# Down projection of a gated decoder block: blocks of 1024 columns, two of eight pairs of k-tiles by Strassen's scheme, the residual in DRAM during the MLP

## The chip, the cores and the metric

The kernel runs on one core of a Trainium2 chip. The metric is the device time of one execution in microseconds. Before the change it is 1585.26 us (median of three runs, 1582.78 to 1585.36). The execution that the profiler recorded took 1583.8 us, and its span, from the first to the last instruction that the profile shows, is 1581.7 us.

## The reference

One decoder layer for 256 tokens of width 2048, all in float32. Its second half, the MLP, is what the change touches; the first half (a combined input projection, three branches with gates, and the projection w_o) ends in the residual `x`.

```
h = RMSNorm_pre(x);  proj = h @ w_in            # conv, short conv, attention query, 3 gates
merged = sum_i sigmoid(gate_i) * y_i            # y_i: a branch's output through its own projection
x = x + RMSNorm_post(merged @ w_o)              # the residual that is kept during the MLP
h = RMSNorm_pre(x)
f = square(relu(h @ w_up)) @ w_down             # w_up 2048 x 8192, w_down 8192 x 2048
x = x + RMSNorm_post(f)
```

## The kernel before

**Precision.** Each float32 operand of a matmul is split into a high part of the type fp32r and a low part (the difference). A product of two tiles takes three matmuls: high by high, high by low, low by high. The split of the activations is made once; the split of the weights is made on the fly for every weight tile, by a copy on ACT into a tile `wh` and a subtraction on DVE into a tile `wl`.

**The weight stream.** All weights pass once, in units of 512 KB, in one fixed order (the list `units`). `fetch_next` issues a unit's DMA on SP into one of six `raw` buffers (`RAW = 6`) and the two instructions that split it into one of five `wh` and five `wl` buffers. `in_unit(u)` fetches up to `LOOK = 4` units ahead of the unit that is being multiplied. A scheduler orders the instructions of each engine when the program is built; the priority of fetches (`PRIO`) and of `soon()` is raised.

**The MLP** runs in four blocks of 2048 of the 8192 hidden columns. In each, four groups of `channels_first` give 512 hidden channels each (the weights are stationary, the tokens move; four PSUM banks per group). DVE and ACT then add the two halves of a bank, apply relu, the norm's factor and the square, and split the result into a tile `ft`. Then four groups of the down projection follow, each of 512 of the 2048 output columns, by `tokens_first`: the tokens are stationary, the weights move, two banks for the two halves of the tokens. `after_down` adds each bank to a sum in SBUF (`acc2`; the first block copies it there on ACT). The last group of the last block is written finer, with the final norm and the output in between.

**Strassen's scheme** is in the kernel already, in `block`, for four of the six gate blocks (`GATES`, with `X_PAIRS`) and for half of w_o (`O_PAIRS`). A block covers 1024 columns, as two halves of 512, and both halves of the tokens, so that each row (a k-tile of 128) takes four products, C11, C12, C21 and C22, in four banks. For a pair of k-tiles it computes seven products in place of eight: P1, P6, P7 and Q5 in four banks of their own, over all pairs of the block, and three that go straight into the C banks. `gather` then adds P1, P6, P7 and Q5 up for the four C results. In the form with pairs the weights of a pair come as four units: "first" and "second" are loaded; "outer" is made from them on DVE by two additions; "inner" is what two accumulating DMAs leave in the buffer of "first", issued on POOL, one after the split of "first" and one after that of "second". `plan_rows` writes out the order of these units among the plain rows, and `TQ` is the order of the four products of a row and of reading out the four C banks.

Of the kernel before, what the change touches and what calls it, by code (L numbers as in the profile page):

```python
# [8 lines left out]
F32 = mybir.dt.float32  # L9
# [6 lines left out]
P = 128  # L16
# [26 lines left out]
X_PAIRS = ((0, 8), (1, 9), (2, 10))  # L43
GATES = ((0, 3), (2, 3), (0, 3))
O_PAIRS = ((0, 4), (1, 5), (2, 6))
TQ = ((0, 1), (0, 0), (1, 1), (1, 0))
LOOK = 4
PRIO = 400
RAW = 6
# [3 lines left out]
def tile_hybrid_block(ctx, tc, x, head, xT, mem, memT, vecs, w_in, w_a_out, w_b_out, w_kv, w_x_out, w_o,  # L53
# [4 lines left out]
    wp = ctx.enter_context(tc.tile_pool(name="wp", bufs=2))  # L58
    big = ctx.enter_context(tc.tile_pool(name="big", bufs=13))
    sm = ctx.enter_context(tc.tile_pool(name="sm", bufs=2))  # L60
    ps = ctx.enter_context(tc.tile_pool(name="ps", bufs=8, space=bass.MemoryType.PSUM))

    uid = [0]

    def name(p):
        uid[0] += 1
        return f"{p}_{uid[0]}"
# [28 lines left out]
            k += s  # L96
        return got

    def plan_rows(w, col0, nk, pairs=(), hold=0):

        taken = [k for p in pairs for k in p]
        rows = [("row", k, None) for k in range(nk) if k not in taken]
        parts = [(4 * j + at, what, k, j) for j, (k0, k1) in enumerate(pairs)
                 for what, k, at in (("first", k0, 0), ("second", k1, 1), ("outer", k0, 4.5), ("inner", k0, 6.5))]
        parts = [p[1:] for p in sorted(parts)]
        order, among = rows[:2], rows[2:-1]
        for n, p in enumerate(parts):
            while n >= hold and among and (len(among) - 0.5) * (len(parts) - hold) >= (len(rows) - 3) * (len(parts) - n):  # L110
                order.append(among.pop(0))
            order.append(p)
        got = []
        for what, k, j in order + among + rows[-1:]:
            units.append((w, k * P, col0, (what, j), None))
            got.append((what, k, j, len(units) - 1))
        return got, pairs

# [162 lines left out]
                    late.pop(0)(acc)  # L281
        return acc

    def block(rows, act, forms=None, sums=None):

        todo = []
        rows, pairs = rows  # L290

        def tile_of(k, t):
            return lambda: [act(k)[:, i, t * P:(t + 1) * P] for i in range(2)]

        def form(j, i):
            return lambda: [f[:, j, i, :] for f in forms]

        for what, k, j, u in rows:
            if what == "row":
# [12 lines left out]
        end = max((i for c, i in last.items() if c[0] != "C"), default=None)  # L312
        acc = {}
        for i, (u, c, a, q) in enumerate(todo):
            wh, wl = in_unit(u)[q]
            ah, al = a()
            first = c not in acc
            if first:
                acc[c] = bank()
            mm(acc[c], ah, wh, first, False)  # L320
            mm(acc[c], ah, wl, False, False)
            mm(acc[c], al, wh, False, i == last[c])
            if i == end:
                with soon():
                    gather(acc, sums)
            if i % 8 == 7:
                between()
        return acc

    def gather(acc, sums):  # L330
        p1, u2 = sums(0, 1), sm.tile([P, NC5], F32, tag="u512", name=name("u"), bufs=2)
        nc.scalar.copy(p1, acc["P1"])
        nc.vector.tensor_tensor(u2, acc["P6"], p1, ALU.add)
        nc.vector.tensor_tensor(sums(1, 1), acc["P7"], u2, ALU.add)
        nc.vector.tensor_tensor(sums(0, 0), acc["Q5"], u2, ALU.subtract)
        nc.vector.tensor_tensor(sums(1, 0), acc["Q5"], sums(1, 1), ALU.subtract)

    def halves(b, dst):
        t = t1k()
# [24 lines left out]

    def lagged(b, w):
        for n in range(2):
            g_gate[b, n] = plan_rows(w_in, C_G + b * D + n * 2 * NC5, KD, X_PAIRS[:GATES[b][n]])
            g_y[b, n] = plan_rows(w, n * 2 * NC5, 8)

    g_sc, g_sx, g_sb = [], [], []  # L370
    lagged(2, w_x_out)
# [3 lines left out]
        g_sb.append(plan(w_in, 0, C_SB + i * NC5))  # L375
    lagged(1, w_b_out)
    lagged(0, w_a_out)
    g_o = [plan_rows(w_o, 0, KD, O_PAIRS, hold=5), None] + [plan(w_o, 0, n * NC5) for n in (2, 3)]
    for blk in range(4):
        for g in range(4):  # L380
            g_up[blk, g] = plan(w_up, 0, blk * D + g * NC5, gain=V_MLP)
        for n in range(4):
            g_dn[blk, n] = plan(w_down, blk * D, n * NC5)


    vec = const.tile([P, V_N], F32, name="vec")
# [255 lines left out]

    def gates(b, n):
        s = t8([P, 2, 2, NC5])
        acc = block(g_gate[b, n], xg, xf, lambda t, q: s[:, t, q, :])
        with soon():
            for t, q in TQ:
                src = acc[f"C{t + 1}{2 - q}"]
                if GATES[b][n]:
                    nc.vector.tensor_tensor(s[:, t, q, :], src, s[:, t, q, :], ALU.add)  # L650
                    src = s[:, t, q, :]
                nc.scalar.activation(s[:, t, q, :], src, AF.Sigmoid, scale=r_of["x"][:, t:t + 1])
        return s
# [169 lines left out]
    def o_part(t, q):  # L823
        return x2[t][:, q * NC5:(q + 1) * NC5]

    acc = block(g_o[0], pair(merged), of, o_part)
    for t, q in TQ:
        nc.vector.tensor_tensor(o_part(t, q), acc[f"C{t + 1}{2 - q}"], o_part(t, q), ALU.add)
        after_o(q, t, o_part(t, q))
# [39 lines left out]


    gq = a_pad.rearrange("p c t -> p (c t)")[:, :D]
    nc.sync.dma_start(gq, g_mlp_post.partition_broadcast(P))
    late_rf = []
    acc2 = [t8([P, D]) for _ in range(2)]

    def after_down(blk, n, t, b, c0=0, c1=NC5):
        b = b[:, :c1 - c0]
        ns = slice(n * NC5 + c0, n * NC5 + c1)
        if blk == 0:
            nc.scalar.copy(acc2[t][:, ns], b)  # L880
            return
        nc.vector.tensor_tensor(acc2[t][:, ns], b, acc2[t][:, ns], ALU.add)
        if blk == 3:
            j = n + (c0 > 0)
            nc.scalar.activation(junk()[:, c0:c1], acc2[t][:, ns], AF.Square, accum_out=ssf[t][:, j:j + 1])
            nc.vector.tensor_tensor(res[t][:, ns], acc2[t][:, ns], gq[:, ns], ALU.mult)

    def finish(t, rf, c0, c1):
        ns = slice(c0, c1)
        nc.vector.scalar_tensor_tensor(res[t][:, ns], res[t][:, ns], rf, x2[t][:, ns], ALU.mult, ALU.add)  # L890
        nc.sync.dma_start(out[t * P:(t + 1) * P, ns], res[t][:, ns])

    for blk in range(4):
        f = []
        for g in range(4):
            first = blk == 0 and g == 0
            if first:
                steps += [stats_2, lambda: over_partitions(r2, r2_bc)]
            banks = channels_first(g_up[blk, g], pair(h2),
                                   late=turns if first else None)  # L900
            ft = t8([P, 4, 2, T], F32R)
            for c, b in enumerate(banks):
                s = t1k()
                halves(b, s)
                nc.vector.scalar_tensor_tensor(s, s, 0.0, r2_bc, ALU.max, ALU.mult)  # L905
                q = t1k()
                nc.vector.tensor_tensor(q, s, s, ALU.mult)  # L907
                split(q, ft[:, c, 0, :], ft[:, c, 1, :])
            f.append(ft)
        if blk == 3:  # L910
            res = [t8([P, D]) for _ in range(2)]
        for n in range(4):
            if blk == 3 and n == 3:
                def none(acc):
                    pass

                def d_0(acc):
                    after_down(3, 3, 0, acc[0])
                    rf = row_rsqrt(ssf[0])
                    for n in range(3):  # L920
                        finish(0, rf, n * NC5, (n + 1) * NC5)
                    late_rf.append(rf)

                def d_1a(acc):
                    after_down(3, 3, 1, acc[1], 0, T)

                def d_1(acc):
                    after_down(3, 3, 1, acc[2], T, NC5)
                    rf = row_rsqrt(ssf[1])
                    with tc.issue_after(mean[0]):  # L930
# [45 lines left out]
```

## Time and profile before

| | value |
|---|---|
| median of 3 runs | 1585.26 us |
| the profiled execution: time, span | 1583.8 us, 1581.7 us |
| busy share of PE, DVE, ACT | 99%, 74%, 51% |
| weights and other data moved | 313.00 MB at a mean of 198 GB/s |
| the MLP | from about 862 us to the end |

PE is the matmul engine, PEld its load of the stationary operand, DVE the vector engine, ACT the scalar engine, POOL and SP the engines that here mostly issue DMAs. A row of a view by windows gives, for a stretch of the span, its length, the busy time of PE, PEld, DVE, ACT and POOL with their instruction counts, the share of full speed of the clock that TensorE was granted, the busy share of the DMA engines, and GB/s. In the view by lines, a group has its busy time, the mean duration in ns of one instruction, and the idle time before them with what ended it. Matmuls overlap, so that the mean duration of one (390 ns) is not its cost; the distance between starts is.

### The profile page before, as it was taken

Reading aid. Unit: us, or ns where it says so; the run is one execution under the profiler, and the core shown is the slowest. Engines: PE = TensorE matmul, PEld = TensorE weight load, DVE = VectorE, ACT = ScalarE, POOL = GpSimd, SP = SyncE. Lnnn points to the kernel's source line nnn. Section 1 sums busy time; section 2 is a strip of 40 time slices with the busy share of each in tenths; the row PEclk is TensorE's granted clock in tenths of the full one; section 3 lists DMA queues with packets and bytes.
Section 4 is the critical chain, followed back from the end, with each engine's and each line's share of the span. In section 5 each row is a group of like instructions: output and inputs, shape, how many; then the busy total and the mean of one; then the engine's idle time right before and its main releaser. Section 6 shows DMA issues by size and latency. Waiting matters only on the chain.

```text
span 1581.7 us, 21250 instructions
## 1 busy us (share of the span) xinstructions
PE 1562.7 (99%) x7908; PEld 1333.9 (84%) x7908; DVE 1164.5 (74%) x1731; ACT 805.8 (51%) x1135; POOL 31.5 (2%) x47
## 2 busy tenths in 40 slices
PE   8999999999999999999999999999999999999997
PEld 7888888888888888888788888888888888888886
DVE  7888787798888987878776775457755676567755
ACT  7654454554443645455455554455534554455542
POOL 0000000000000010000100000000000000000000
PEclk9999999999999999999999999999999999999999
DMA  9765655577666768558775766666556665666562
GB/s 315 223 205 191 189 162 172 160 232 220 186 189 173 237 187 281 183 175 239 225 255 160 213 187 192 195 194 192 187 190 197 188 191 192 190 194 190 188 196 82
DMA packets 142248, 313.00 MB, mean 198 GB/s; under 512 B 9920, under 2 KB 14272, under 8 KB 141632
## 3 DMA queue, kind: packets, MB, share of 16 engines
q1 hardware_dynamic: 138112, 304.30, 61.3%
q0 software_dynamic: 4032, 7.34, 2.7%
q8 instruction: 62, 1.02, 0.3%
q14 instruction: 42, 0.34, 0.1%
HBM read 302.17 MB, written 2.10 MB: 192 GB/s over the span
## 4 chain that ended last, share of the span: by engine, by line
PE 91%; DMA 3%; DVE 3%; issue 2%; ACT 0%; SPq 0%; POOL 0%; POOLq 0%; DVEq 0%; ACTq 0%
PE bank L82 91%; DMA raw<-raw 2%; DVE wl L145 1%; DMA raw<-in_w_in 1%; DMA raw<-in_w_o 0%; DVE t L811 0%; PE bank L769 0%; ACT wh L144 0%; DVE t L665 0%; DVE t L650 0%; DVE t L890 0%; DVE t L345 0%; DVE raw L137 0%; DVE wl L167 0%; PE bank L819 0%
## 5 line engine op out<-in xcount | busy, mean ns | idle before, releaser
L82 PE MATMUL bank<-wh,t 128*128 128x512 f32 (+1 forms) x2564 | 787.5, 387 | 0.0
L82 PEld LDWEIGHTS bank<-wh,t 128*128 128x128 f32 x2564 | 479.8, 188 | 97.1
L82 PE MATMUL bank<-wl,t 128*128 128x512 f32 (+1 forms) x1282 | 496.2, 387 | 0.1
L162 DVE TENSOR_TENSOR wl<-raw,wh 128x1024 fp32r<-128x1024 f32 (+1 forms) x273 | 332.4, 1220 | 208.3 <-ACT wh L161 207.7
L82 PE MATMUL bank<-t,wh 128*128 128x512 f32 (+1 forms) x1936 | 464.1, 390 | 5.8 <-ACT wh L161 4.6
L161 ACT CAST wh<-raw 128x1024 fp32r<-128x1024 f32 (+1 forms) x273 | 286.1, 1049 | 332.2 <-PE bank L82 314.7
L82 PEld LDWEIGHTS bank<-t,wh 128*128 128x128 f32 x1936 | 354.3, 189 | 73.6 <-ACT wh L161 4.6
L144 ACT CAST wh<-raw 128x1024 fp32r<-128x1024 f32 (+1 forms) x188 | 189.4, 1020 | 190.1 <-PE bank L82 117.1
L82 PEld LDWEIGHTS bank<-wl,t 128*128 128x128 f32 x1282 | 241.1, 188 | 49.3 <-DVE wl L145 1.0
L82 PEld LDWEIGHTS bank<-t,wl 128*128 128x128 f32 x1936 | 249.5, 192 | 10.3 <-DVE wl L162 0.7
L82 PE MATMUL bank<-t,wl 128*128 128x256 f32 (+1 forms) x1936 | 252.8, 283 | 0.4 <-DVE wl L162 0.4
L145 DVE TENSOR_TENSOR wl<-raw,wh 128x1024 fp32r<-128x1024 f32 (+1 forms) x188 | 217.8, 1180 | 45.0 <-ACT wh L144 44.3
L167 DVE SCALAR_TENSOR_TENSOR wl<-raw,vec,wh 128x512 fp32r<-128x512 f32 x256 | 180.7, 747 | 78.7 <-ACT wh L166 78.4
L166 ACT ACTIVATE wh<-raw,vec 128x512 fp32r<-128x512 f32 x256 | 171.4, 717 | 106.6 <-PE bank L82 80.3
L574 DVE SCALAR_TENSOR_TENSOR t<-a_pad,vec,t 128x256 f32<-128x256 f32 x240 | 103.6, 478 | 0.0
L340 ACT COPY s<-bank 128x256 f32<-128x256 f32 x128 | 45.8, 366 | 56.0 <-PE bank L82 54.6
L341 DVE TENSOR_TENSOR s<-bank,s 128x256 f32<-128x256 f32 x128 | 51.9, 419 | 20.0 <-ACT s L340 20.0
L344 ACT CAST t<-s 128x256 fp32r<-128x256 f32 x96 | 37.7, 401 | 29.6 <-DVE s L907 21.9
L345 DVE TENSOR_TENSOR t<-s,t 128x256 fp32r<-128x256 f32 x96 | 39.5, 419 | 1.8
L907 DVE TENSOR_TENSOR s<-s 128x256 f32<-128x256 f32 x64 | 27.1, 424 | 1.8
L905 DVE SCALAR_TENSOR_TENSOR s<-s,rm_bc 128x256 f32<-128x256 f32 x64 | 27.0, 422 | 1.4
L439 POOL TENSOR_TENSOR y<-y,mhalf 128x1 f32<-128x1 f32 (+1 forms) x7 | 4.8, 681 | 937.2 <-DVE y L437 937.2
(127 smaller groups left out, 432.7 us busy)
## 6 DMA issues: line engine op xcount, KB each, us to landing
raw<-in_w_in SPq DMA_DIRECT2D x191, 512.0 KB, 4.3
raw<-in_w_up SPq DMA_DIRECT2D x128, 512.0 KB, 3.8
raw<-in_w_down SPq DMA_DIRECT2D x128, 512.0 KB, 4.0
raw<-in_w_kv SPq DMA_DIRECT2D x32, 512.0 KB, 4.5
raw<-in_w_o SPq DMA_DIRECT2D x32, 512.0 KB, 5.3
raw<-in_w_x_out SPq DMA_DIRECT2D x16, 512.0 KB, 4.3
raw<-in_w_b_out SPq DMA_DIRECT2D x16, 512.0 KB, 5.5
raw<-in_w_a_out SPq DMA_DIRECT2D x16, 512.0 KB, 5.0
```

The lines of the kernel that those rows point to most:

```text
L82: nc.tensor.matmul(o, a, b, start=start, stop=stop)
L144: nc.scalar.copy(h[:, part], raw[:, part])
L145: pace[0] = nc.vector.tensor_tensor(l[:, part], raw[:, part], h[:, part].bitcast(F32), ALU.subtract).ins
L161: nc.scalar.copy(h, raw)
L162: pace[0] = nc.vector.tensor_tensor(l, raw, h.bitcast(F32), ALU.subtract).ins
L166: nc.scalar.mul(h[:, j, :], raw[:, j, :], g)
L167: pace[0] = nc.vector.scalar_tensor_tensor(l[:, j, :], raw[:, j, :], g, h[:, j, :].bitcast(F32), ALU.mult, ALU.subtract).ins
L340: nc.scalar.copy(t, b[:, T:])
L341: nc.vector.tensor_tensor(dst, b[:, :T], t, ALU.add)
L344: nc.scalar.copy(dst_h, src)
L345: nc.vector.tensor_tensor(dst_l, src, dst_h.bitcast(F32), ALU.subtract)
L574: nc.vector.scalar_tensor_tensor(conv[:, c, :], src, w, conv[:, c, :], ALU.mult, ALU.add)
```

## The change

In the first three blocks of the MLP both halves of the output columns, and in the fourth block the first half, go through `block` with two pairs of k-tiles each (`D_PAIRS`), so seven blocks of 1024 columns. The plan puts four plain rows ahead of the pairs (`lead=4`). The second half of the last block stays as it was. The sums for the pairs that the activations need (`down_sums`) are made while the second up group of each block is read out; for this two squared tiles of the first group are kept, and their split form takes a large buffer `fd`. To make room, the residual `x2` is written to DRAM at the start of the MLP and read back in the last block. `gather_add` does what `gather` does and adds to `acc2`, which all blocks after the first need. `TQ` changes for every block of the kernel: it now goes through the two halves of the tokens first.

```diff
-TQ = ((0, 1), (0, 0), (1, 1), (1, 0))
+D_PAIRS = ((0, 4), (1, 5))
+TQ = ((0, 0), (1, 0), (0, 1), (1, 1))
...
-    def plan_rows(w, col0, nk, pairs=(), hold=0):
+    def plan_rows(w, row0, col0, nk, pairs=(), lead=2, hold=0):
...
-        order, among = rows[:2], rows[2:-1]
+        order, among = rows[:lead], rows[lead:-1]
...
+    def gather_add(acc, sums):
+        p1, u3 = t512(), t512()
+        nc.scalar.copy(p1, acc["P1"])
+        nc.vector.tensor_tensor(sums(0, 1), acc["P1"], sums(0, 1), ALU.add)
+        nc.vector.tensor_tensor(p1, acc["P6"], p1, ALU.add)
+        nc.vector.tensor_tensor(u3, acc["P7"], p1, ALU.add)
+        nc.vector.tensor_tensor(p1, acc["Q5"], p1, ALU.subtract)
+        nc.vector.tensor_tensor(sums(1, 1), sums(1, 1), u3, ALU.add)
+        nc.vector.tensor_tensor(u3, acc["Q5"], u3, ALU.subtract)
+        nc.vector.tensor_tensor(sums(0, 0), sums(0, 0), p1, ALU.add)
+        nc.vector.tensor_tensor(sums(1, 0), sums(1, 0), u3, ALU.add)
...
-        for n in range(4):
-            g_dn[blk, n] = plan(w_down, blk * D, n * NC5)
+        for n in range(2):
+            if blk < 3 or n == 0:
+                g_dn[blk, n] = plan_rows(w_down, blk * D, n * 2 * NC5, KD, D_PAIRS, lead=4)
+    for n in (2, 3):
+        g_dn[3, n] = plan(w_down, 3 * D, n * NC5)
...
+    def keep_x2():
+        for t in range(2):
+            nc.sync.dma_start(x2_kept[t], x2[t])
...
-        if blk == 0:
-            nc.scalar.copy(acc2[t][:, ns], b)
-            return
...
+    def down_sums(fd, j, qa, qb):
+        s = t512().rearrange("p (i t) -> p i t", i=4)
+        nc.vector.tensor_tensor(s[:, 0, :], qa[:, P:], qb[:, P:], ALU.subtract)
+        nc.vector.tensor_tensor(s[:, 1, :], s[:, 0, :], qa[:, :P], ALU.subtract)
+        nc.vector.tensor_tensor(s[:, 2, :], qa[:, :P], qa[:, P:], ALU.subtract)
+        nc.vector.tensor_tensor(s[:, 3, :], qb[:, :P], s[:, 1, :], ALU.add)
+        split(s, fd[:, 0, j], fd[:, 1, j])
...
+                steps += [stats_2, lambda: over_partitions(r2, r2_bc), keep_x2, load_gq]
...
+                if g == 0 and paired:
+                    kept.append(q)
+                elif g == 1 and paired:
+                    down_sums(fd, c, kept[c], q)
...
         if blk == 3:
             res = [t8([P, D]) for _ in range(2)]
-        for n in range(4):
-            if blk == 3 and n == 3:
+            for t in range(2):
+                x2[t] = t8([P, D])
+                nc.sync.dma_start(x2[t], x2_kept[t])
+        forms = [fd[:, i] for i in range(2)]
+        for n in range(2 if blk < 3 else 1):
+            def part(t, q):
+                return acc2[t][:, (2 * n + q) * NC5:(2 * n + q + 1) * NC5]
+            acc = block(g_dn[blk, n], pair(f), forms,
+                        lambda acc: gather(acc, part) if blk == 0 else gather_add(acc, part))
+            for t, q in TQ:
+                after_down(blk, 2 * n + q, t, acc[f"C{t + 1}{2 - q}"])
+        for n in (2, 3) if blk == 3 else ():
+            if n == 3:
```

The units of one new block stand in this order: four plain rows, first 0, a row, second 0, a row, first 1, a row, outer 0, a row, second 1, inner 0, a row, outer 1, a row, inner 1, two rows.

Three places in the order of the instructions. On DVE, where the down projection of the second block ends and the next block's up projection begins, this stood before (`wl` with `vec` is the split of a w_up unit, L882 the addition of a bank to the sum):

```order
L162 TENSOR_TENSOR wl_10735<-raw_10732,wh_10734 128x1024
L162 TENSOR_TENSOR wl_10753<-raw_10750,wh_10752 128x1024
L167 SCALAR_TENSOR_TENSOR wl_10771<-raw_10768,vec,wh_10770 128x512 x2
L167 SCALAR_TENSOR_TENSOR wl_10791<-raw_10788,vec,wh_10790 128x512 x2
L167 SCALAR_TENSOR_TENSOR wl_10811<-raw_10808,vec,wh_10810 128x512 x2
L167 SCALAR_TENSOR_TENSOR wl_10831<-raw_10828,vec,wh_10830 128x512 x2
L882 TENSOR_TENSOR t_1438_7706<-bank_10694,t_1438_7706 128x512
L882 TENSOR_TENSOR t_1439_7707<-bank_10695,t_1439_7707 128x512
```

And now, at the same place, with `gather_add` in lines 349 to 355 (bank_10847 is P6, bank_10893 P7, bank_10889 Q5; wl_10900 and wl_10917 are the block's last two rows):

```order
L147 TENSOR_TENSOR wl_10900<-raw_10897,wh_10899 128x1024
L349 TENSOR_TENSOR u_10961<-bank_10847,u_10961 128x512
L147 TENSOR_TENSOR wl_10918<-raw_10915,wh_10917 128x1024
L169 SCALAR_TENSOR_TENSOR wl_10930<-raw_10927,vec,wh_10929 128x512 x2
L169 SCALAR_TENSOR_TENSOR wl_10950<-raw_10947,vec,wh_10949 128x512
L350 TENSOR_TENSOR u_10962<-bank_10893,u_10961 128x512
L169 SCALAR_TENSOR_TENSOR wl_10950<-raw_10947,vec,wh_10949 128x512
L351 TENSOR_TENSOR u_10961<-bank_10889,u_10961 128x512
L352 TENSOR_TENSOR t_1439_7710<-t_1439_7710,u_10962 128x512
L354 TENSOR_TENSOR t_1438_7709<-t_1438_7709,u_10961 128x512
L353 TENSOR_TENSOR u_10962<-bank_10889,u_10962 128x512
L169 SCALAR_TENSOR_TENSOR wl_10975<-raw_10972,vec,wh_10974 128x512
```

The reads of P7 and Q5, after which their banks can be written again, stand among the splits of the next up group's first units, and L353 is the last of them.

On SP, in the first up group of the MLP, the DMAs stood so before:

```order
L157 DMA raw_7820<-in_w_up 128x2x512
L157 DMA raw_7844<-in_w_up 128x2x512
L872 DMA a_pad<-in_g_mlp_post 128x2048
L157 DMA raw_7894<-in_w_up 128x2x512
L157 DMA raw_7918<-in_w_up 128x2x512
```

Now two writes of 1 MB each (`x_kept`) stand among them:

```order
L159 DMA raw_7824<-in_w_up 128x2x512
L902 DMA x_kept_7707<-t_1282_6956 128x2048
L159 DMA raw_7848<-in_w_up 128x2x512
L896 DMA a_pad<-in_g_mlp_post 128x2048
L902 DMA x_kept_7708<-t_1284_6959 128x2048
L159 DMA raw_7898<-in_w_up 128x2x512
```

The w_up units behind them are issued later by those two transfers.

On PE, at the start of w_o (from about 773 us), the transposes of the merged branches (`ident`; bank_7011 and bank_7018) stood in two pieces before:

```order
L82 MATMUL bank_7003<-wh_6889,t_1197_6520 128x512
L769 MATMUL bank_7011<-ident,t_654_3545 128x128
L769 MATMUL bank_7018<-ident,t_654_3545 128x128
L82 MATMUL bank_7032<-wh_6907,t_1181_6454 128x512
L82 MATMUL bank_7032<-wl_6908,t_1181_6454 128x512
L82 MATMUL bank_7032<-wh_6907,t_1181_6454 128x512
L769 MATMUL bank_7011<-ident,t_654_3545 128x128 x3
L769 MATMUL bank_7018<-ident,t_654_3545 128x128 x3
```

Now all eight stand together, at the place of the first piece:

```order
L84 MATMUL bank_7005<-wh_6891,t_1197_6522 128x512
L791 MATMUL bank_7013<-ident,t_654_3547 128x128 x4
L791 MATMUL bank_7020<-ident,t_654_3547 128x128 x4
L84 MATMUL bank_7034<-wh_6909,t_1181_6456 128x512
L84 MATMUL bank_7034<-wl_6910,t_1181_6456 128x512
L84 MATMUL bank_7034<-wh_6909,t_1181_6456 128x512
```

With the new `TQ` both halves of the tokens of these columns are read out before the other columns, and the second piece has moved up to the first.

## Rows read from the trace of the kernel before

**Rows 1.** The page: busy time of the engines, and the chain by engine.

```profile
PE 1562.7 (99%) x7908; PEld 1333.9 (84%) x7908; DVE 1164.5 (74%) x1731; ACT 805.8 (51%) x1135; POOL 31.5 (2%) x47
PE 91%; DMA 3%; DVE 3%; issue 2%; ACT 0%; SPq 0%; POOL 0%; POOLq 0%; DVEq 0%; ACTq 0%
```

**Rows 2.** Windows: two paired gate blocks, an up group, a down group.

```profile
312.10:353.60 41.50, 41.44 (x183) 33.99 (x182) 37.49 (x54) 22.50 (x23) 4.47 (x6) 1.00 0.79 226
582.00:623.50 41.50, 41.45 (x184) 33.98 (x183) 36.99 (x39) 24.46 (x27) 2.61 (x3) 1.00 0.86 271
...
922.00:945.00 23.00, 23.00 (x133) 20.29 (x132) 17.78 (x35) 13.02 (x24) 0.00 (x0) 1.00 0.62 195
...
967.00:988.80 21.80, 21.80 (x98) 18.06 (x97) 10.23 (x10) 9.50 (x10) 0.00 (x0) 1.00 0.60 195
```

**Rows 3.** PE in order of time, down projection: start, length, instructions.

```profile
1000.05 0.62 PE L82 MATMUL bank<-wh,t 128*128 128x512 f32 x2
...
1000.73 0.62 PE L82 MATMUL bank<-wh,t 128*128 128x512 f32 x2
```

**Rows 4.** Groups by line and shape: count, busy us, mean ns, idle before.

```profile
L145 DVE TENSOR_TENSOR wl<-raw,wh 128x1024 fp32r<-128x1024 f32 x174 | 208.7, 1220 | 42.9 <-ACT wh L144 42.2
L144 ACT CAST wh<-raw 128x1024 fp32r<-128x1024 f32 x174 | 181.0, 1052 | 167.1 <-PE bank L82 97.4 <-issue 23.0 <-DVE raw L137 15.2
L167 DVE SCALAR_TENSOR_TENSOR wl<-raw,vec,wh 128x512 fp32r<-128x512 f32 x256 | 180.7, 747 | 78.7 <-ACT wh L166 78.4
...
L882 DVE TENSOR_TENSOR t<-bank,t 128x512 f32<-128x512 f32 x23 | 14.9, 683 | 5.9 <-PE bank L82 5.9
...
L145 DVE TENSOR_TENSOR wl<-raw,wh 128x512 fp32r<-128x512 f32 x14 | 9.6, 685 | 2.1 <-ACT wh L144 2.1
L137 DVE TENSOR_TENSOR raw<-raw,raw 128x512 f32<-128x512 f32 x14 | 9.6, 685 | 0.0
...
L447 DVE TENSOR_SCALAR s<-ident,y 128x128 f32<-128x128 f32 x8 | 2.0, 284 | 2.3 <-POOL y L439 1.6 <-POOL y L868 0.7
```

**Rows 5.** The chain in order of time, in the gate block from 312 us.

```profile
325.78 3.56 DMA raw<-in_w_in
329.38 6.16 DMA raw<-raw
...
337.51 243.16 PE bank L82 x1251
```

**Rows 6.** DMAs: the median us to landing is the last number.

```profile
raw<-raw POOLq DMA_DIRECT2D x28, 256.0 KB, 4.1
...
t<-in_x SPq DMA_DIRECT2D x2, 1024.0 KB, 8.8
```

**Rows 7.** The tile raw in the gate block from 312 us: its DMAs.

```profile
DMA to landing us min/median/max: 3.5/4.7/6.2
```

**Rows 8.** PE in order of time at the start of w_o: start, length, wait.

```profile
773.61 0.39 PE L82 MATMUL bank<-wh,t 128*128 128x512 f32 x1
775.55 0.44 PE L769 MATMUL bank<-ident,t 128*128 128x128 f32 x2 [1.55 <-DVE t L665]
...
777.48 1.54 PE L769 MATMUL bank<-ident,t 128*128 128x128 f32 x6 [0.79 <-DVE t L665]
```

**Rows 9.** DVE in order of time at the same place.

```profile
774.82 1.28 DVE L665 TENSOR_TENSOR t<-t,t 128x512 f32<-128x512 f32 x2
...
776.73 0.69 DVE L665 TENSOR_TENSOR t<-t,t 128x512 f32<-128x512 f32 x1
```

**Rows 10.** Windows: the start of w_o, and the start of the MLP.

```profile
777.40:780.80 3.40, 3.32 (x11) 2.94 (x12) 3.40 (x5) 1.59 (x3) 0.61 (x1) 0.50 0.81 193
...
860.00:870.00 10.00, 8.88 (x72) 8.31 (x70) 9.93 (x19) 9.84 (x25) 0.56 (x1) 1.00 0.45 160
```

**Rows 11.** PE's waits at the start of the MLP, in order of time.

```profile
857.60 0.66 PE L819 MATMUL bank<-ident,t 128*128 128x128 f32 x4 [0.54 <-DVE t L811]
...
865.60 0.63 PE L819 MATMUL bank<-ident,t 128*128 128x128 f32 x4 [1.12 <-DVE t L811]
```

More of the change, by code (lines that the diff above doesn't have):

```diff
@@ L60, in tile_hybrid_block @@
     sm = ctx.enter_context(tc.tile_pool(name="sm", bufs=2))
+    dram = ctx.enter_context(tc.tile_pool(name="dram", bufs=1, space=bass.MemoryType.DRAM))
     ps = ctx.enter_context(tc.tile_pool(name="ps", bufs=8, space=bass.MemoryType.PSUM))
@@ L107, in plan_rows @@
         parts = [p[1:] for p in sorted(parts)]
-        order, among = rows[:2], rows[2:-1]
+        order, among = rows[:lead], rows[lead:-1]
         for n, p in enumerate(parts):
-            while n >= hold and among and (len(among) - 0.5) * (len(parts) - hold) >= (len(rows) - 3) * (len(parts) - n):
+            while n >= hold and among and (len(among) - 0.5) * (len(parts) - hold) >= (len(rows) - 1 - lead) * (len(parts) - n):
                 order.append(among.pop(0))
@@ L114, in plan_rows @@
         for what, k, j in order + among + rows[-1:]:
-            units.append((w, k * P, col0, (what, j), None))
+            units.append((w, row0 + k * P, col0, (what, j), None))
             got.append((what, k, j, len(units) - 1))
@@ L282, in tokens_first, with block @@
         return acc
-    def block(rows, act, forms=None, sums=None):
+    def block(rows, act, forms=None, gathered=None):
         todo = []
@@ L324, in block @@
                 with soon():
-                    gather(acc, sums)
+                    gathered(acc)
             if i % 8 == 7:
@@ L328, in block, with t512 @@
         return acc
+    def t512():
+        return sm.tile([P, NC5], F32, tag="u512", name=name("u"), bufs=3)
     def gather(acc, sums):
-        p1, u2 = sums(0, 1), sm.tile([P, NC5], F32, tag="u512", name=name("u"), bufs=2)
+        p1, u2 = sums(0, 1), t512()
         nc.scalar.copy(p1, acc["P1"])
@@ L366, in lagged @@
         for n in range(2):
-            g_gate[b, n] = plan_rows(w_in, C_G + b * D + n * 2 * NC5, KD, X_PAIRS[:GATES[b][n]])
-            g_y[b, n] = plan_rows(w, n * 2 * NC5, 8)
+            g_gate[b, n] = plan_rows(w_in, 0, C_G + b * D + n * 2 * NC5, KD, X_PAIRS[:GATES[b][n]])
+            g_y[b, n] = plan_rows(w, 0, n * 2 * NC5, 8)
     g_sc, g_sx, g_sb = [], [], []
@@ L377, in tile_hybrid_block @@
     lagged(0, w_a_out)
-    g_o = [plan_rows(w_o, 0, KD, O_PAIRS, hold=5), None] + [plan(w_o, 0, n * NC5) for n in (2, 3)]
+    g_o = [plan_rows(w_o, 0, 0, KD, O_PAIRS, hold=5), None] + [plan(w_o, 0, n * NC5) for n in (2, 3)]
     for blk in range(4):
@@ L644, in gates @@
         s = t8([P, 2, 2, NC5])
-        acc = block(g_gate[b, n], xg, xf, lambda t, q: s[:, t, q, :])
+        acc = block(g_gate[b, n], xg, xf, lambda acc: gather(acc, lambda t, q: s[:, t, q, :]))
         with soon():
@@ L824, in o_part @@
         return x2[t][:, q * NC5:(q + 1) * NC5]
-    acc = block(g_o[0], pair(merged), of, o_part)
+    acc = block(g_o[0], pair(merged), of, lambda acc: gather(acc, o_part))
     for t, q in TQ:
@@ L871, in tile_hybrid_block, with load_gq @@
     gq = a_pad.rearrange("p c t -> p (c t)")[:, :D]
-    nc.sync.dma_start(gq, g_mlp_post.partition_broadcast(P))
+    def load_gq():
+        nc.sync.dma_start(gq, g_mlp_post.partition_broadcast(P))
+    x2_kept = [dram.tile([P, D], F32, tag=f"x2{t}", name=f"x2_kept{t}") for t in range(2)]
+    def keep_x2():
+        for t in range(2):
+            nc.sync.dma_start(x2_kept[t], x2[t])
     late_rf = []
@@ L891, in finish @@
         nc.sync.dma_start(out[t * P:(t + 1) * P, ns], res[t][:, ns])
+    def down_sums(fd, j, qa, qb):
[5 more added lines that the diff above has]
+        split(s, fd[:, 0, j], fd[:, 1, j])
     for blk in range(4):
-        f = []
+        f, kept = [], []
+        fd = t8([P, 2, len(D_PAIRS), 4, P], F32R)
         for g in range(4):
@@ L897, in tile_hybrid_block @@
             if first:
-                steps += [stats_2, lambda: over_partitions(r2, r2_bc)]
+                steps += [stats_2, lambda: over_partitions(r2, r2_bc), keep_x2, load_gq]
             banks = channels_first(g_up[blk, g], pair(h2),
@@ L905, in tile_hybrid_block @@
                 nc.vector.scalar_tensor_tensor(s, s, 0.0, r2_bc, ALU.max, ALU.mult)
-                q = t1k()
+                paired = c < len(D_PAIRS)
+                q = (sm.tile([P, T], F32, tag="kept", name=name("q"), bufs=len(D_PAIRS)) if g == 0 and paired else t1k())
                 nc.vector.tensor_tensor(q, s, s, ALU.mult)
                 split(q, ft[:, c, 0, :], ft[:, c, 1, :])
+                if g == 0 and paired:
+                    kept.append(q)
+                elif g == 1 and paired:
+                    down_sums(fd, c, kept[c], q)
             f.append(ft)
```

## The prediction

> **What bounds the kernel now.** I read the page first: PE is busy 99% of the span, and PE is 91% of the chain [rows 1]. A busy PE need not be a PE at its rate, so next the matmuls in order of time. In the down projection the same place in the pattern of three matmuls returns after 0.68 us (1000.05 to 1000.73) [rows 3]: one matmul of 512 columns each 0.227 us, with the granted clock at 1.00, the 2.4 GHz level [rows 2]. So the MLP is a queue of matmuls without holes, and a matmul that is left out is time gained, as long as the other engines keep up. In a down group DVE works 10.23 of 21.80 us, in an up group 17.78 of 23.00, and the weights come at 195 GB/s, where 226 and 271 GB/s were moved in other stretches [rows 2].
>
> The kernel contains its own experiment for the change: two gate blocks of 1024 columns with three pairs each. There PE worked 41.44 and 41.45 of 41.50 us, with DVE at 37.49 and 36.99 [rows 2]. The scheme ran without loss where DVE was 90% busy, since the convolution's taps lay there too.
>
> **The change part by part.**
>
> Matmuls. A pair saves one product of eight, three matmuls. Seven blocks with two pairs: 42 matmuls x 0.227 = **-9.5 us**. A block is 186 matmuls, 42.2 us.
>
> The Trainium skill ("TensorE: Matmul & The Clock Gate", section "Back-to-back issue gap") gives about 131 ns for a matmul of 512 columns in a stream of loads and matmuls, and about 216 ns for one alone. By 131 the 42 would be worth 5.5 us, by 216 9.1 us. The measured distance of 227 ns lies near the second and far from the first, and decides.
>
> DVE in a block. Twelve rows x 1.22 = 14.6 us; a pair splits a half (0.69) and three full units (3.66) and makes "outer" with two additions (1.37), 5.7 us, 11.4 for two; `gather_add` has eight additions and `after_down` four, 12 x 0.683 = 8.2 [rows 4]. Sum 34.3 of 42.2 us, 81%, below the 90% of the gate block that lost nothing. ACT adds 1.5 splits per pair of 1.05 us [rows 4] and has room. PE covers this; without the cover it would be up to the difference to two down groups, 34.3 - 20.5 = 13.8 us per block, which needs PE to wait for all of it. I take 0.06 us per block from the gate block: **+0.4 us**, bounds 0 and (for a DVE late by some us at each end) 7.
>
> The sums for the pairs. 2 x (4 x 0.284 + 0.683) = 3.6 us of DVE in one up group of four [rows 4]: 17.78 + 3.6 = 21.4 of 23.0. The converted weights give a cushion: with five buffers a unit's split starts when PE is done with the unit five before, so four units of 2.72 us (four products of 0.68) before its use, less 1.05 and 1.22 for the split: 8.6 us. I cost it 0, bounds 0 and 3.6 x 4 = 14 if DVE had no slack left at all.
>
> The waits inside a block. "outer" and "inner" wait for accumulating DMAs, 28 more on POOL, of a median 4.1 us [rows 6], 3.5 to 6.2 in the gate block [rows 7]. A wait on DVE holds the splits of the following units behind it, and PE waits for those. In the gate block the chain went through a weight load (3.56), an accumulation (6.16) and a split, and PE took over at 337.51 without a hole to speak of [rows 5]: the cushion was just used up. "outer" needs what "first" has sent, "inner" also what "second" has. Counted in products of 0.68 us, the tightest of these distances are 10.9 us (first to outer) and 9.5 (second to inner) in the new order, and 8.2 and 6.8 in the gate block; four rows stand ahead instead of two, and there are two pairs, not three. So 0, in the 0.4 above; bounds in the rivals.
>
> The banks at a block's end. All eight banks are in use, and the next up group starts on the four of P1, P6, P7 and Q5 at once. P7 is complete two rows before the end, 8 x 0.68 = 5.4 us; its last reader is L353. On DVE five additions and half a split of w_up stand from there to L353, 5 x 0.683 + 0.747 = 4.2 us [rows 4]. The fourth bank is written three matmuls after the group's start, so 5.4 + 0.7 - 4.2 = 1.9 us are left. Cost 0. Behind a late L353 the splits of the third w_up unit and all later ones stand queued. Between two paired blocks the banks are wanted one by one each 1.36 us, which is easier.
>
> The residual. Two writes of 1 MB and two reads; a read of 1 MB took 8.8 us [rows 6]. The writes stand in SP's queue beside the first up group's weights, together with 1 MB that was there before. The DMA engines are 45% busy from 860 us on [rows 10], and a unit's `raw` buffer is free six units before it is wanted by the split, so two more MB at 200 to 270 GB/s (8 to 10 us) are within 6 x 2.72 = 16 us. In the last block the two target buffers are those of earlier hidden tiles, and the residual is used only at the end. Cost 0, bounds 0 and 8.
>
> The new `TQ`. It reaches beyond the MLP. At the start of w_o PE waits 1.55 and then 0.79 us for the read-out of the last branch block (L665), which releases the transposes [rows 8]. The four read-outs end over 2.7 us; the first piece starts when the second and third are being added (774.82), the second piece when the last is done (776.73 + 0.69) [rows 9]. With both halves of the tokens of the first 512 columns read out ahead, all eight transposes need only what is added by 775.5. The first wait stays, the second goes: **-0.8 us**. Behind these waits the granted clock was 0.50, the 1.2 GHz level, from 777.4 to 780.8 [rows 10]: 3.4 us at half speed, 1.7 us lost. At the start of the MLP PE waited 0.54 and 1.12 us [rows 11], 1.66 in sum, and the clock stayed at 1.00 [rows 10]. What is left at w_o, 1.55, is nearer to that than to 2.34, so I take the whole **-1.7 us**, with 0 as the other bound.
>
> **Sum.** 1583.8 - 9.5 + 0.4 - 0.8 - 1.7 = 1572.2 us for an execution like the profiled one. The median of the runs is 1.5 us above it; with that 1573.7 us.
>
> **The rivals.**
> (a) DVE late at the block ends, or accumulations a little late, so that a third to three quarters of the gain goes: 0.5 to 1 us in each of seven blocks, 3.5 to 7 us, gives 1577 to 1581. For it: the gate block's cushion fell to nothing, and `gather_add` is longer than `gather`. Against: DVE has 8 us free in a block.
> (b) The other side. The accumulating DMAs pace the blocks: "outer" and "inner" stand on DVE until they have landed, with the splits of all later units behind them. It decides from the point where the way from a split through the accumulation to the next split takes longer than the distance plus the cushion, 9.5 + 8.6 = 18 us; in the gate block 6.8 + 8.6 = 15 us were just used up. Were it 19.2 us, each of the 14 pairs would cost 1.2 us, 17 us in all, and the time would be 1591. Against: the worst landing in the gate block was 6.2 us with 226 GB/s beside it, and the down projection moves 195.
> The Trainium skill ("SBUF — State Buffer", section "Who interferes with whom") says that a DVE instruction with two inputs in SBUF and a GpSimd instruction that reads SBUF exclude each other. This speaks for (b), since the splits are such instructions and the DMAs are issued there; the landings of 3.5 to 6.2 us beside a DVE that was 90% busy bear out no more than what is in the sum.
> (c) The change doesn't do what it says: the MLP is paced by something other than matmuls, and with 42 fewer PE waits 9.5 us more for weights. Then only `TQ` counts, and the time is 1583 to 1585. Against: 195 GB/s is no limit seen here, and ACT's splits wait for PE, not PE for them.
> (d) The clock still falls at w_o: +1.7, so 1575.4, within the likeliest case.
>
> **How the numbers follow.** The likeliest case, with the clock either way and up to 3 us lost in the blocks: 65%, 1571.5 to 1577. More gained than that (the first wait at w_o shrinks too): 5%, 1569 to 1571.5. (a) 18%, (c) 5%, (b) 7%. The range for 8 of 10 leaves out (b), (c) and some of the better end: 1570 to 1581. What can be told from no change is about 0.2%, 3.2 us: faster means below 1582. Nearly all of the likeliest and better cases and of (a) lie there: 0.86; (c) and the rest of (a): 0.08; (b) and a little more: 0.06.
>
> **What would show it.** In the profile after: 42 fewer matmuls of 512 columns on L84 at the same distance of 0.227 us; PE at 100% in windows over the seven blocks, each 42.2 us long; DVE at about 34 of them; no wait of an up group's first matmuls for L353; at the start of w_o one wait instead of two and a clock of 1.00. I would be wrong if PE had holes of more than 0.5 us per block ahead of "outer" or "inner" (then (b), by its size (a)), or at the block ends, or if matmuls stood further apart than before.

## The result, and the profile after

The changed kernel takes **1574.55 us** (median of four runs, 1573.12 to 1575.26) against 1584.02 us for the kernel before on the same chip: a ratio of 0.994, 95% interval 0.9923 to 0.9957. It was forecast at 1573.7 us. The profiled execution took 1574.08 us, its span is 1572.2 us, 9.5 us less than before.

The page of the changed kernel shows the busy time, POOL's DMA queue, the chain, and the accumulating DMAs with their median us to landing. They answer to [rows 1, 6].

```profile
PE 1551.4 (99%) x7866; PEld 1324.9 (84%) x7866; DVE 1245.8 (79%) x1883; ACT 831.5 (53%) x1170; POOL 55.6 (4%) x75
...
q0 software_dynamic: 8064, 14.68, 5.4%
...
PE 91%; DMA 3%; DVE 3%; issue 2%; ACT 0%; POOL 0%; SPq 0%; POOLq 0%; DVEq 0%; ACTq 0%
...
raw<-raw POOLq DMA_DIRECT2D x56, 256.0 KB, 3.7
```

There are 42 matmuls fewer, and 81 us more of DVE's work beside them. The windows below, as in [rows 2] and [rows 10], are the first two paired down blocks, the paired block of the last block row, and a stretch each at the MLP's start and at w_o's.

```profile
955.68:997.84 42.16, 42.16 (x187) 34.91 (x186) 34.02 (x46) 22.74 (x28) 3.47 (x4) 1.00 0.70 214
997.84:1040.00 42.16, 42.16 (x187) 34.91 (x186) 30.16 (x36) 21.65 (x25) 3.44 (x4) 1.00 0.75 223
1475.84:1518.00 42.16, 41.65 (x184) 34.17 (x183) 32.60 (x45) 22.62 (x28) 3.44 (x4) 1.00 0.82 250
863.70:867.10 3.40, 3.40 (x20) 3.40 (x20) 3.40 (x6) 3.13 (x11) 0.00 (x0) 0.57 0.83 347
777.40:780.80 3.40, 3.40 (x18) 2.80 (x17) 3.40 (x4) 1.53 (x3) 0.00 (x0) 1.00 0.83 222
```

A block lasts 42.16 us, in the first six PE never stops, and DVE works 34.02 us in the first. Half speed is gone from w_o and stands at the MLP's start. PE in order of time at these two places, only the rows with a wait; they answer to [rows 8] and [rows 11].

```profile
774.17 0.99 PE L791 MATMUL bank<-ident,t 128*128 128x128 f32 x7 [1.67 <-DVE t L687]
784.62 0.63 PE L791 MATMUL bank<-ident,t 128*128 128x128 f32 x4 [1.03 <-DVE t L364]
...
855.16 0.66 PE L841 MATMUL bank<-ident,t 128*128 128x128 f32 x4 [0.54 <-DVE t L833]
863.16 0.63 PE L841 MATMUL bank<-ident,t 128*128 128x128 f32 x4 [1.15 <-DVE t L833]
```

The second wait for the read-out (0.79 us) is gone, but ten microseconds later the next turn's transposes wait 1.03 us. The one hole in the seven blocks (a time in which PE stands idle) lies in the last. The chain there, in order of time (start, length, what):

```profile
1478.01 9.14 DMA raw<-raw
...
1491.24 6.66 DMA raw<-raw
...
1498.59 1.23 DVE wl L147
...
1499.87 2.34 PE bank L84 x9
```

An accumulating DMA took 9.14 us, where the slowest of [rows 7] took 6.2. SP had issued the two reads of the residual, 1 MB each, just before:

```profile
1475.05 0.90 SPq L957 DMA_DIRECT2D t<-x_kept  x2
```

Where the 9.5 us came from can be added up from the distances between starts of matmuls in both traces (time beyond the undisturbed distance): 42 matmuls -9.5; the MLP's blocks +0.9, of it 0.8 in the hole at 1499.87; w_o's start -0.8; the MLP's start +1.4; the gate blocks -0.8 and the first 12 us -0.9, in stretches where the change alters at most an order; the end +0.3.

### The profile page after: what moved, and what is told of

Same layout as the page of the kernel before. It is cut to its first block, busy times and chain, and to the rows that moved or that the text cites. A ratio compares the mean times of both kernels' runs of the same rounds, so it can differ in the third digit from the quotient of the medians.

```text
span 1572.2 us, 21520 instructions
## 1 busy us (share of the span) xinstructions
PE 1551.4 (99%) x7866; PEld 1324.9 (84%) x7866; DVE 1245.8 (79%) x1883; ACT 831.5 (53%) x1170; POOL 55.6 (4%) x75
## 4 chain that ended last, share of the span: by engine, by line
PE 91%; DMA 3%; DVE 3%; issue 2%; ACT 0%; POOL 0%; SPq 0%; POOLq 0%; DVEq 0%; ACTq 0%
PE bank L84 90%; DMA raw<-raw 2%; DVE wl L147 1%; DMA raw<-in_w_o 1%; DMA t<-in_xT 0%; DMA raw<-in_w_down 0%; DVE t L833 0%; DVE t L364 0%; DVE raw L139 0%; DVE t L672 0%; PE bank L841 0%; ACT wh L146 0%; DVE t L918 0%; DVE wl L169 0%; DVE t L687 0%
## 5 line engine op out<-in xcount | busy, mean ns | idle before, releaser
L84 PE MATMUL bank<-wh,t 128*128 128x512 f32 (+1 forms) x2536 | 778.2, 387 | 0.0
L84 PEld LDWEIGHTS bank<-wh,t 128*128 128x128 f32 x2536 | 474.0, 188 | 96.6 <-DVE t L364 0.5
L146 ACT CAST wh<-raw 128x1024 fp32r<-128x1024 f32 (+1 forms) x328 | 330.2, 1017 | 330.7 <-PE bank L84 246.0
L84 PE MATMUL bank<-wl,t 128*128 128x512 f32 (+1 forms) x1268 | 490.4, 387 | 0.5 <-DVE wl L147 0.5
L147 DVE TENSOR_TENSOR wl<-raw,wh 128x1024 fp32r<-128x1024 f32 (+1 forms) x328 | 379.6, 1176 | 95.8 <-ACT wh L146 93.7
L163 ACT CAST wh<-raw 128x1024 fp32r<-128x1024 f32 (+1 forms) x161 | 168.1, 1046 | 165.7 <-PE bank L84 152.6
L164 DVE TENSOR_TENSOR wl<-raw,wh 128x1024 fp32r<-128x1024 f32 (+1 forms) x161 | 195.5, 1217 | 73.7 <-ACT wh L163 73.2
L149 POOL DMA_DIRECT2D raw<-raw x28 | 24.4, 872 | 1025.3 <-DVE wl L147 1014.5
L363 ACT CAST t<-s 128x256 fp32r<-128x256 f32 x88 | 34.2, 401 | 37.7 <-DVE s L946 29.4
L138 DVE TENSOR_TENSOR raw<-raw,raw 128x512 f32<-128x512 f32 x28 | 19.3, 689 | 28.3 <-DMA raw<-raw 27.1
L364 DVE TENSOR_TENSOR t<-s,t 128x256 fp32r<-128x256 f32 x88 | 36.3, 421 | 5.0 <-ACT t L363 3.8
L151 POOL DMA_DIRECT2D raw<-raw x28 | 24.2, 863 | 127.1 <-DMA raw<-raw 108.8
```

Source lines behind the costliest of these rows:

```text
L84: nc.tensor.matmul(o, a, b, start=start, stop=stop)
L146: nc.scalar.copy(h[:, part], raw[:, part])
L147: pace[0] = nc.vector.tensor_tensor(l[:, part], raw[:, part], h[:, part].bitcast(F32), ALU.subtract).ins
L163: nc.scalar.copy(h, raw)
L164: pace[0] = nc.vector.tensor_tensor(l, raw, h.bitcast(F32), ALU.subtract).ins
L363: nc.scalar.copy(dst_h, src)
```

## Experiments

**The new `TQ` alone, and the change without it.** The first is the kernel before with the new line, the second the changed kernel with the old one.

```
-TQ = ((0, 1), (0, 0), (1, 1), (1, 0))
+TQ = ((0, 0), (1, 0), (0, 1), (1, 1))
```

> The kernel before with the new order TQ alone. Theory: the down projection's gain is its 42 matmuls and TQ is worth about 1.5 us, 0.8 at the start of w_o (the transposes wait once, not twice) and 0.7 in the two gate blocks whose small holes (0.33 and 0.32 us at 337 and 602 us) were gone in the changed kernel; so a ratio to before of 0.999, and the MLP as long as before. The half-speed stretch of the clock (3.4 us) still occurs once, at w_o or at the start of the MLP. Rival: the 1.7 us of that stretch are won as well, then 3 us, 0.998. Rival two: TQ carries a large share of the change, 4 us or more, 0.997 or lower.

> The changed kernel with the old order TQ. Theory: the seven blocks keep 42.16 us each, the two waits at the start of w_o come back (1.7 and 1.0 us between matmuls), and the time is 1 to 2 us above the changed kernel, 8 us below before, ratio 0.995. Rival: the old order also lets the banks of a block come free later for its neighbour (the C banks of one half of the columns are read out last), so holes at the block ends of 0.5 to 1 us each, 4 to 6 us above the changed kernel.

Measured: the new `TQ` alone 1582.31 us, ratio 0.9991 (0.9983 to 1.0), 1.4 us, hardly to be told from nothing. The change without it 1575.03 us, 0.9949 (0.9935 to 0.9963), which the interval of the full change holds. The windows at w_o and at the MLP's start, of the first and then of the second kernel:

```profile
777.40:780.80 3.40, 3.40 (x17) 2.81 (x16) 3.40 (x5) 2.25 (x4) 0.00 (x0) 1.00 0.85 205
863.70:867.10 3.40, 3.18 (x26) 3.05 (x27) 3.40 (x7) 3.40 (x12) 0.00 (x0) 1.00 0.71 243
```

```profile
777.40:780.80 3.40, 3.40 (x18) 2.84 (x16) 3.40 (x5) 2.58 (x4) 0.00 (x0) 1.00 0.85 210
863.70:867.10 3.40, 3.01 (x25) 2.88 (x26) 3.40 (x6) 3.40 (x12) 0.00 (x0) 1.00 0.84 351
```

With the old order the clock stayed at 1.00 too, behind waits of 1.32 and 0.79 us. So the stretch at half speed is not bound to the second wait. Nor is the order worth anything at w_o when the clock stays up: by the distances between starts, the same 300 matmuls there took 70.6 us before, 69.8 with the new order (alone, and in the change), and 69.6 in the change with the old order. The first expectation's 1.5 us is met in the number, not by its reason. The gate blocks gain 0.7 of their 0.8 us in the run with the old order too.

**The residual read later.** In the last block row the reads are issued behind the paired block.

```
         if blk == 3:
             res = [t8([P, D]) for _ in range(2)]
-            for t in range(2):
-                x2[t] = t8([P, D])
-                nc.sync.dma_start(x2[t], x2_kept[t])
...
         for n in (2, 3) if blk == 3 else ():
+            if n == 2:
+                for t in range(2):
+                    x2[t] = t8([P, D])
+                    nc.sync.dma_start(x2[t], x2_kept[t])
```

> The changed kernel with the residual read back behind the paired block of the last MLP block instead of ahead of it. Theory: the 0.79 us hole of PE at 1499.87 comes from the two reads of 1 MB, which stand in SP's queue in the middle of that block and stretch its accumulations to 9.1 us; without them there PE's cushion stays at 2 us or more, the hole goes, and the time is 0.8 us less than the changed kernel's. Rival: the hole comes from the last block's other work and stays, or the reads now delay the weights of the fine last groups, and the time is the same or up to 2 us more.

Measured: 1574.1 us, 0.9942 (0.993 to 0.9955). The hole is gone: from 950 us to 1560 PE has no wait left that the trace shows, and the least time from a split's end to its first matmul in the last block is 4.2 us instead of 0.1. The last block's four accumulating DMAs land in 3.3 to 4.5 us, where two took 9.1 and 6.7. The reads made the hole. Its 0.8 us are too few for the medians to show.

**Three pairs, with accumulating DMAs.** `D_PAIRS` gets a third pair; the second of these runs also reads the residual late.

```
-D_PAIRS = ((0, 4), (1, 5))
+D_PAIRS = ((0, 4), (1, 5), (2, 6))
```

> The changed kernel with three pairs in each of the seven blocks in place of two (the kept squares share a buffer of the attention, the third pair's sums take a second large buffer). Theory: 21 more matmuls saved, 4.8 us, and the cushion of the converted weights, 2.2 us at its lowest in the changed kernel's first six blocks, carries a DVE at about 90%: ratio to before 0.991. Rival: the accumulations and DVE pace the blocks from here; each block loses 0.7 us or more to holes ahead of outer and inner units, the gain is given back, ratio 0.994 or higher.

> Three pairs with accumulating DMAs, and the residual read back behind the paired block of the last block row: the run with VectorE's sums, but for who adds the halves of w_down. Theory 'the accumulating DMAs': the holes of 1 to 4.3 us per block and the fallen clock stay as in the first run with three pairs, at most the last block's is smaller: 1590 to 1598 us. Rival 'what helped was the late read': holes gone, 1568 to 1572 us.

Measured: **slower than before**, 1598.29 us, 1.0095 (1.0081 to 1.0108), and with the late read 1593.51, 1.0064 (1.0045 to 1.0083). PE's waits from 950 us to 1560 in the first run (total us, times, longest):

```profile
PE bank L84 <- DVE wl L147: 16.3, 7, 4.2
```

DVE in its first paired block, before and at the third pair's "outer":

```profile
978.22 1.23 DVE L147 TENSOR_TENSOR wl<-raw,wh 128x1024 fp32r<-128x1024 f32 x1 [0.28 <-ACT wh L146]
985.89 0.69 DVE L138 TENSOR_TENSOR raw<-raw,raw 128x512 f32<-128x512 f32 x1 [6.45 <-DMA raw<-raw]
```

"outer" (L138) stands 6.45 us on DVE until the accumulation has landed, with the later splits behind it. PE ran dry for 3.02 us, and the clock fell (first PE's row behind the hole, then a window):

```profile
987.77 0.79 PE L84 MATMUL bank<-wl,t 128*128 128x512 f32 x1 [3.02 <-DVE wl L147]
```

```profile
987.80:994.00 6.20, 6.20 (x15) 4.89 (x16) 6.17 (x6) 2.94 (x3) 0.00 (x0) 0.52 0.77 225
```

The late read makes the last block's hole smaller (4.2 us to 2.6), but the holes of the other blocks stay and the kernel is still slower than before. In its run 17.3 us of waits and four stretches of 3.4 us at half speed (6.6 us lost, by the distances between starts) make up 23.9 of the 24.5 us that separate it from the same kernel with sums on VectorE, below.

**Two pairs, the accumulations doubled.** A DMA that adds zeros goes ahead of each.

```
+        if w is w_down and what == "first":
+            nc.gpsimd.dma_start(raw[:, 1], zeros, accum_op=ALU.add)
+        elif w is w_down and what == "second":
+            nc.gpsimd.dma_start(held["first", j][:, 0], zeros, accum_op=ALU.add)
...
```

> The changed kernel, with every accumulating DMA of the down projection preceded by one more that adds a tile of zeros into the same half (28 more, of 256 KB each); the pieces that the first block row leaves are kept in another buffer, as in the run with three pairs. Theory 'the cushion carries the accumulations': before a block's next tile is needed 2.2 to 4.5 us are left in the first six blocks and 0.1 us in the last; a second landing of 3.5 to 4.7 us ahead of each sum uses that up once or twice per block, so holes of TensorE ahead of an outer row in most blocks, 0.5 to 3 us each, 1577 to 1592 us. Theory 'the rows between give room enough': no hole but the one in the last block, which grows by at most 4 us: 1574 to 1578 us.

Measured: 1633.86 us, 1.0319 (1.0304 to 1.0334), beyond both. The second pair's DMAs in the first block, POOL in order of time; each waits for the one before to land:

```profile
971.46 1.16 POOL L149 DMA_DIRECT2D raw<-zeros  x1
976.59 0.86 POOL L153 DMA_DIRECT2D raw<-raw  x1 [3.97 <-DMA raw<-zeros]
984.14 0.86 POOL L151 DMA_DIRECT2D raw<-zeros  x1 [6.69 <-DMA raw<-raw]
```

From the first issue to the landing that "outer" needs it is now 12.7 us. The same pair in the changed kernel:

```profile
968.41 0.86 POOL L149 DMA_DIRECT2D raw<-raw  x1 [5.28 <-DVE wl L147]
974.70 0.86 POOL L151 DMA_DIRECT2D raw<-raw  x1 [5.43 <-DMA raw<-raw]
```

There it was 6.3 us, and the least time left behind it between a split and its first matmul 2.4 us. From these a hole of 12.7 - 6.3 - 2.4 = 4.0 us is to be expected; the one at 986.55 is 3.5. The whole run, by lines, and a window that begins in the second block's hole:

```profile
L84 PE MATMUL bank<-wl,t 128*128 128x512 f32 x1236 | 488.7, 395 | 39.0 <-DVE wl L147 38.9
```

```profile
1033.00:1043.00 10.00, 4.59 (x11) 3.64 (x12) 7.06 (x7) 3.56 (x4) 1.72 (x2) 0.50 0.58 126
```

PE is idle 39.0 us before L147's tiles. Five stretches in the MLP, 41 us in all, stand at half speed, but PE is idle in much of them (it works 4.59 of the 10.00 us in the window), so that they don't cost the half of their length. By the distances between starts the holes cost 45.8 us, the half speed 11.0 and smaller delays 3.5, in sum 60.3; the changed kernel has 1.1 in the same stretch, and the medians differ by 59.3.

**Two rows ahead in place of four.** `lead=4` becomes 2.

> The changed kernel with two plain rows ahead of the pairs in a down block, as in the other blocks, in place of four. If the four rows are what holds the cushion, the outer rows come some 2 x 3.6 = 7 us earlier and the sums before them are late by 7 less the cushion of 2.2 to 4.5 us: holes of 2 to 4 us in each of seven blocks, 1588 to 1600 us. If the order of the parts behind them gives the room, no holes but the one in the last block: 1573.5 to 1576 us.

Measured: 1575.21 us, 0.9951 (0.9938 to 0.9963). I had expected holes in every block; the one of note is in the last, 1.2 us, beside the residual's reads. Elsewhere at least 2.3 us were left between a split and its first matmul, as with four rows (2.2). My first theory falls: what is left is not a matter of the rows ahead.

**Three pairs, the sums of the halves on VectorE or on GpSimd**, with the late read. The second has `nc.gpsimd` in place of `nc.vector`.

```
-        if what == "first":
+        if w is w_down and what in ("first", "second"):
+            to, by = (raw[:, 1], raw[:, 0]) if what == "first" else (held["first", j][:, 0], raw[:, 0])
+            nc.vector.tensor_tensor(to, to, by, ALU.add)
+        elif what == "first":
...
```

> Three pairs in the down blocks, the residual read back behind the paired block of the last block row, and the sums of w_down's halves on VectorE (two adds of 128x512 for each pair, 0.685 us each) in place of the accumulating DMAs. Theory 'three pairs are slow by the accumulating DMAs and by the clock that falls after the holes they make': no holes, the clock at 1.00 in the blocks, 21 matmuls fewer (-4.8 us) on the 1574 of the run with the late read: 1568 to 1571 us. Rival 'three pairs are too much for VectorE itself': it had 32.7 of 41 us busy with three pairs and gets 6 x 0.685 = 4.1 us more per block, 90%; holes of 1 to 4 us per block stay and the clock falls as it did: 1585 to 1600 us.

> As the run with VectorE's sums, but the sums of w_down's halves on GpSimd. No row of this kernel has an add on GpSimd; were it to take as long as an accumulating DMA's landing (3.5 us and more), the holes would be those of three pairs with accumulating DMAs, 1590 to 1598 us. If it takes under 2 us, the theory of the accumulating DMAs gives 1568 to 1571 us, as on VectorE; if GpSimd's adds slow VectorE's instructions beside them, VectorE's mean for a 128x1024 cast rises over 1.22 us and holes stay.

Measured: on VectorE **1569.04 us**, 0.9907 (0.9894 to 0.992), the fastest version; on GpSimd 1573.67, 0.9942 (0.993 to 0.9954). Windows of the first, early in two blocks:

```profile
957.00:998.00 41.00, 41.00 (x182) 33.96 (x181) 37.39 (x51) 23.34 (x30) 0.00 (x0) 1.00 0.57 187
1129.00:1170.00 41.00, 41.00 (x182) 33.95 (x182) 37.81 (x52) 23.44 (x31) 0.00 (x0) 1.00 0.56 189
```

DVE does 42 additions more and is 91 to 92% busy, and PE does not wait. So it was the landing of the DMAs that made three pairs slow, not DVE's load and not the reads. Against two pairs with the late read it gains 5.1 us, where 21 matmuls make 4.8. With GpSimd, a place in the first block, its rows and then DVE's:

```profile
979.71 1.29 POOL L150 TENSOR_TENSOR raw<-raw 128x512 f32<-128x512 f32 x1 [7.96 <-DVE wl L147]
981.08 1.79 POOL L150 TENSOR_TENSOR raw<-raw,raw 128x512 f32<-128x512 f32 x1
```

```profile
981.03 0.69 DVE L138 TENSOR_TENSOR raw<-raw,raw 128x512 f32<-128x512 f32 x1 [1.40 <-POOL raw L150]
981.76 1.66 DVE L139 TENSOR_TENSOR raw<-raw,raw 128x512 f32<-128x512 f32 x1
```

Here L139 takes 1.66 us beside GpSimd's addition, 0.69 without. Seven of the 21 in the down blocks, one in each block, take over 1.5 us, and L138 waits for GpSimd's additions as well. PE has four holes of 0.8 to 1.0 us. GpSimd's additions took under 2 us in the median, so of the expectation's cases it was the third, VectorE slowed, mainly in L139 (925 ns in the mean, 686 in the change; the splits' mean is 1.23 us against 1.22).

**Four pairs, the sums on VectorE.** As the version above, with (3, 7).

> As the run with three pairs and VectorE's sums, but four pairs of eight. Theory 'the matmuls are the term, 0.227 us each, as long as VectorE keeps up': 21 more matmuls gone, -4.8 us on 1569.0: 1563 to 1566 us; VectorE gets one pair's work more per block (two adds of a half, two of an outer row, two splits in three, some 3 us net of the rows that go) and stands at 36 to 38 of some 40.8 us. Rival 'VectorE is the bound from here': an outer row's split is late by 1 to 4 us in the blocks, the clock falls behind the holes, 1570 to 1600 us.

Measured: 1584.72 us, 1.0006 (0.9998 to 1.0015): all of the gain is lost. PE's waits from 950 us to 1560, and DVE in the first block:

```profile
PE bank L84 <- DVE wl L147: 3.1, 8, 0.5
PE bank L84 <- ACT wh L146: 2.2, 9, 0.4
PE bank L84 <- DVE t L913: 2.0, 2, 1.0
```

```profile
957.00:997.00 40.00, 39.36 (x171) 31.52 (x170) 36.88 (x54) 22.92 (x31) 0.00 (x0) 1.00 0.46 152
```

The window shows DVE at 92%, as with three pairs, though it has more to do per block. By the prediction's working a pair costs DVE 5.7 + 1.4 = 7.1 us and takes two rows' 2.4 away: 41.7 us per block with three pairs (a block is 41.5), 46.4 with four (40.8). My expectation had 3 us net per pair; it is 4.7. Of the 3.1 us in which DVE is idle in this window 2.4 are waits for ACT. The longest stands behind the two additions of an "outer", until ACT has copied what DVE just made:

```profile
992.30 2.36 DVE L147 TENSOR_TENSOR wl<-raw,wh 128x1024 fp32r<-128x1024 f32 x2 [1.18 <-ACT wh L146]
```

How much of the loss is DVE's work, and how much this turn through ACT, no run here separates. The clock did not fall here: by the distances between matmuls, 19.8 us more are lost than with three pairs, 19.5 of it in small waits from 950 us on, against 4.8 gained. That is 15.0 of the 15.7 us.

## Why the prediction was right, and where it was not

The time was right to 0.9 us, and the sign. Some of that closeness is luck: the forecast gain was 11.6 us, from a median before of 1585.26, and the measured gain is 9.5, from 1584.02. By its steps:

- *42 matmuls x 0.227 = -9.5.* Right: 42 fewer, and 42.16 us per block for 42.2. This term alone is the result.
- *DVE in a block, 34.3 us.* The room was right, with PE without holes in six of seven blocks. That the first window shows 34.02 is chance: it holds 6.8 us of the last up group's read-out, and `gather` with four additions instead of `gather_add` with eight. The windows of the seven blocks run from 30.2 to 34.3 us, each with work of its neighbours. *The banks at a block's end*: right, no up group's first matmuls wait.
- *The waits inside a block, 0.* Right for six blocks. But the room is smaller than "9.5 + 8.6 = 18 us" in rival (b): the 8.6 are there when a block starts (8.8, or 7.2 behind another block), and in the pairs DVE draws them down to 2.2 to 4.2 us. At a way of 6.3 us from issue to landing 2.4 were left, so by these numbers it decides from some 8.7 us on, 10 with the two additions of "outer". Rival (b) was real and nearer than its 7% said: one more pair, or a landing of 9 us, reaches it. The argument against it, a worst landing of 6.2 us, took the first of the two gate blocks. The chain of the kernel before had a longer one in the second, where it cost PE some 0.3 us:

```profile
590.32 9.68 DMA raw<-raw
```

- *The residual. Cost 0, bounds 0 and 8.* Mis-sized: 0.8 us. I asked whether the weights would be late and whether the residual would; what was late was an accumulating DMA beside the reads.
- *The second wait at w_o, -0.8.* This step failed: the wait went, but 1.03 us came at the next transposes (in the change with the old order 0.43). The place gained 0.8 us in all, not 2.5, and that is the clock's, since with the clock at 1.00 the old order was no slower there (69.6 us for the 300 matmuls, against 69.8).
- *The clock, -1.7.* This step failed. Its reason was that PE's waits at w_o were too long for 1.00. After the change 1.67 us of wait kept the clock there, and 1.15 us at the MLP's start were followed by 3.4 us at half speed. Without the old second wait, and with it, the two runs on `TQ` show none at either place; the three-pair kernels on VectorE and on GpSimd and the doubled accumulations show one at w_o again. A single stretch of this kind in one profile is no property of the kernel. Why it comes in one execution and not in another stays open.

The two misses, +1.4 of clock and +0.8 of hole, were covered by 1.6 us in the gate blocks and at the start, which I had not forecast. The order is not their cause, since the gate blocks gain with the old one too. No experiment here explains them; they seem to be differences between two executions.

The prediction weighed a rule of the Trainium skill ("SBUF — State Buffer", section "Who interferes with whom") on VectorE instructions with two SBUF inputs beside GpSimd instructions that read SBUF. Issuing DMAs on POOL brings none of it, so that it did not speak for (b): L139 and L147 keep 686 and 1222 ns with twice as many. An addition on GpSimd does: L139's 1.66 us agree with the rule.

## What to carry to other kernels

When the matmul engine is full, price an algorithmic saving by the distance between matmuls in that stage, and then look at the buffer of converted weights at its tightest place, not at its size when the stage begins. A DMA that a vector instruction waits for blocks the queue behind it: if the vector engine has the time, do a small addition there rather than by an accumulating DMA (here 0.69 us against a median of 3.7 and up to 9.1). That held up to three pairs here, and no longer with four. Large transfers that nobody waits for are moved out of stretches in which somebody waits for small ones.

## What the hardware showed that I had not expected

- Accumulating DMAs of 256 KB within SBUF, 3.7 us in the median, took up to 6.6 us in the first six down blocks and 9.1 us with two reads of 1 MB beside them. One of 9.7 us stands in a gate block of the kernel before, where no such reads are.
- In the variants with accumulating DMAs that were slower than before, between a fifth and three tenths of the loss in the blocks is the clock (7.8 of 27.2 us, 6.6 of 27.4 and 11.0 of 60.3, by the distances between starts). Of their 17 holes of TensorE of more than 2 us, 13 went with a fall of the clock to 0.50, for 3.4, 6.8 or 10.2 us; four, of 2.2 to 3.5 us, did not. The waits of 0.3 to 1.2 us of the four-pair kernel, more in number, left it at 1.00.
